# Tiles of three rows in four slots instead of four rows in three slots, in an instance norm that streams 2 GB through one core

## The chip, the core and the metric

One core of a Trainium2 chip runs the kernel alone. The metric is the device time of one execution in microseconds (us); less is better. "Median" is the median of a kernel's runs.

## The reference

```python
x: [256, 256, 4096] float32          # 65536 rows of 4096
mean = np.mean(x, axis=2, keepdims=True)
var = np.var(x, axis=2, keepdims=True)
out = (x - mean) / np.sqrt(var + eps)
```

Each row of 16 KB is read once (1073.74 MB in all), normalized and written once (1073.74 MB). There is no matrix product.

## The kernel before

A tile has 128 partitions with K = 4 consecutive rows each: 64 KB per partition, 8 MB in all, 128 tiles. The kernel keeps three such tiles ("slots") in SBUF. SyncE issues all DMAs, VectorE does the row sums and most scalings, ScalarE the squares, the square roots and three quarters of each tile's last row. This is the part that the change touches, cut:

```python
K = 4; BUFS = 3; Q = 3072
X = [pool.tile([P, K, d], fp32, name=f"x{s}") for s in range(BUFS)]

def vector_tile(s, r0=0, k=K, ...):
    take(V, ld, 16)                                  # the tile has landed
    for r in range(r0, r0 + k):                      # row sums (and x <- x/d)
        V.tensor_scalar(out=x[:, r, :], in0=x[:, r, :], scalar1=1.0 / d, ..., accum_out=mean[s][:, r:r+1]).then_inc(means, 1)
    for b in range(r0, r0 + k, 2):                   # two rows at a time
        ...                                          # wait for their square root
        mine(V.reciprocal(out=rstd..., in_=std...)); mine(V.scalar_tensor_tensor(out=nbias..., ...))
        for r in range(b, b + 2):                    # scale; of the last row only the columns from Q on
            f = slice(Q, d) if r == r0 + k - 1 else slice(0, d)
            V.tensor_scalar(out=x[:, r, f], in0=x[:, r, f], scalar1=rstd..., scalar2=nbias..., ...).then_inc(dn, 1)

def scalar_tile(s, r0=0, k=K, ...):
    for r in range(r0, last + 1):
        mine(A.activation(out=junk, in_=x[:, r, :], func=AF.Square, ..., accum_out=ss[s][:, c]))
        if (r - r0) % 2:                             # a square root for every two rows
            A.activation(out=std..., in_=ss..., func=AF.Sqrt, ...).then_inc(stds, 1)
    A.activation(out=x[:, last, :Q], in_=x[:, last, :Q], func=AF.Identity, ...).then_inc(dn, 1)
...
    # SyncE; the first and the last tile go in halves (cut)
    with S.Fori(0, rounds) as i:
        for t in range(L0, L0 + BUFS):
            store(t % BUFS, (t, BUFS, rounds, i))                 # waits until tile t is done
            load((t + 2) % BUFS, (t + 2, BUFS, rounds, i))        # waits until tile t-1 has been stored
```

The whole kernel:

## Time and profile before

| | before |
|---|---|
| median of the first 6 runs | 4963.06 us (4961.5 to 4963.66) |
| span of the profile | 4960.2 us |
| DMA queue: packets, share of the span | 37296, 100.0% |
| VectorE, ScalarE busy | 66%, 49% |
| one tile, from its load's landing to its store's issue | 26.4 us |

This is the timeline of the kernel before, in two cuts (start, duration, engine, line of the kernel, operation, output and input, count; then the idle time ahead of it and what ended it):

```profile
1004.27 0.34 SPq L165 DMA_DIRECT2D out_dram<-x  x1
1004.85 0.35 SPq L170 DMA_DIRECT2D x<-in_x_dram  x1
1016.84 4.42 DVE L87 TENSOR_SCALAR_CACHE_REDUCE x<-x 128x4096 f32<-128x4096 f32 x1 [12.72 <-DMA x<-in_x_dram]
...
1043.28 0.34 SPq L165 DMA_DIRECT2D out_dram<-x  x1
```

A load lands and the first sum starts at 1016.84; the tile's store is issued at 1043.28, 26.4 us later. Tiles follow each other every 38.6 us, so VectorE is idle for some 12 us of each.

### The profile page before, as it was taken

How to read it: one execution, taken by the hardware profiler on the slowest of the kernel's cores; microseconds unless marked ns; L12 is line 12 of the kernel's file. 1: busy time of each engine (PE TensorE's matmuls, PEld its weight loads, DVE VectorE, ACT ScalarE, POOL GpSimd, SP SyncE). 2: the span in 40 equal slices, each digit the busy share in tenths (PEclk: the TensorE clock that was granted, in tenths of full speed). 3: DMA queues.
4: the chain of work that ended last, by engine and by line, in shares of the span. 5: the costliest groups of instructions: out<-in, count | busy, mean ns of one | idle time of the engine just before them, and what ended most of it. 6: DMA issues, size and time to landing. Idle time of an engine off the chain costs nothing.

```text
span 4960.2 us, 5938 instructions
## 1 busy us (share of the span) xinstructions
DVE 3298.0 (66%) x2049; ACT 2407.7 (49%) x1412; POOL 0.2 (0%) x4
## 2 busy tenths in 40 slices
DVE  6666666666666666666666666666666666666666
ACT  4455444554445544455445544455444554445544
POOL 0000000000000000000000000000000000000000
DMA  9999999999999999999999999999999999999999
GB/s 422 431 435 433 431 435 433 432 437 432 432 438 432 433 437 432 433 437 432 435 435 432 436 434 431 438 433 431 438 433 432 438 432 433 438 432 433 438 432 405
DMA packets 37298, 2147.52 MB, mean 433 GB/s; under 512 B 4144, under 2 KB 4144, under 8 KB 4144
## 3 DMA queue, kind: packets, MB, share of 16 engines
q1 hardware_dynamic: 37296, 2147.50, 100.0%
q14 instruction: 2, 0.02, 0.0%
HBM read 1073.74 MB, written 1073.74 MB: 433 GB/s over the span
## 4 chain that ended last, share of the span: by engine, by line
DVE 62%; another core or an unknown queue 31%; issue 4%; DMA 2%; ACT 0%; DVEq 0%; ACTq 0%; SPq 0%
DVE x L87 44%; DVE x L112 17%; DMA x<-in_x_dram 1%; DVE nbias L100 1%; DMA out_dram<-x 1%; DVE rstd L98 1%; ACT junk L137 0%; DVEq L68 0%; DVEq L219 0%; ACT L146 0%; ACT std L146 0%; ACTq L68 0%; ACTq L67 0%; SPq L265 0%
## 5 line engine op out<-in xcount | busy, mean ns | idle before, releaser
L87 DVE TENSOR_SCALAR_CACHE_REDUCE x<-x 128x4096 f32<-128x4096 f32 x512 | 2232.3, 4416 | 1580.4 <-DMA x<-in_x_dram 1580.4
L137 ACT ACTIVATE junk<-x,mean 128x4096 f32<-128x4096 f32 x512 | 1883.1, 3678 | 2367.2 <-DVE x L87 2367.2
L112 DVE TENSOR_SCALAR x<-x,rstd,nbias 128x4096 f32<-128x4096 f32 (+1 forms) x512 | 1004.2, 2004 | 33.9 <-DVE nbias L100 29.3
L151 ACT ACTIVATE x<-x,nbias,rstd 128x3072 f32<-128x3072 f32 x130 | 383.2, 2948 | 146.2 <-DVEq L68 146.2
L137 ACT ACTIVATION_READ_ACCUMULATOR junk<-x,mean 128x1 f32 x512 | 95.5, 187 | 0.0
L146 ACT ACTIVATE std<-ss,eps_tile 128x2 f32<-128x2 f32 x256 | 75.6, 295 | 19.1
L98 DVE RECIPROCAL rstd<-std 128x2 f32<-128x2 f32 x256 | 40.7, 159 | 19.4 <-ACT std L146 19.4
L100 DVE SCALAR_TENSOR_TENSOR nbias<-mean,rstd 128x2 f32<-128x2 f32 x256 | 41.1, 161 | 8.9
L87 DVE DVE_READ_ACCUMULATOR x<-x 128x1 f32 x512 | 42.3, 83 | 0.0
L137 ACT ACT_TABLE_LOAD x1 | 1.3, 1283 | 1.2 <-DVE eps_tile L216 1.2
L146 ACT ACT_TABLE_LOAD x1 | 1.3, 1283 | 0.1
L216 DVE MEMSET eps_tile<- 128x1 f32 x1 | 0.1, 59 | 1.0 <-SPq L192 1.0
L251 POOL MEMSET const-bfloat16-1.0<- 128x1 bf16 x1 | 0.1, 101 | 0.0
L251 POOL MEMSET const-uint8-127<- 128x1 uint8 x1 | 0.1, 101 | 0.0
L251 POOL MEMSET const-float32-1.0<- 128x1 f32 x1 | 0.1, 99 | 0.0
L251 POOL MEMSET const-float32-0.0<- 128x1 f32 x1 | 0.1, 98 | 0.2 <-issue 0.2
## 6 DMA issues: line engine op xcount, KB each, us to landing
out_dram<-x SPq DMA_DIRECT2D x4, 4096.0 KB, 19.6
x<-in_x_dram SPq DMA_DIRECT2D x2, 4096.0 KB, 16.7
x<-in_x_dram SPq DMA_DIRECT2D x127, 50.3
out_dram<-x SPq DMA_DIRECT2D x126, 31.5
```

What stands on the lines that cost most here:

```text
L87: V.tensor_scalar(out=x[:, r, :], in0=x[:, r, :], scalar1=1.0 / d, scalar2=None, op0=ALU.mult, op1=ALU.add, accum_out=mean[s][:, r : r + 1 ...
L98: mine(V.reciprocal(out=rstd[s][:, c], in_=std[s][:, c]))
L100: mine(V.scalar_tensor_tensor(out=nbias[s][:, c], in0=mean[s][:, c], scalar=-1.0 / d, in1=rstd[s][:, c], op0=ALU.mult, op1=ALU.mult))
L112: V.tensor_scalar(out=x[:, r, f], in0=x[:, r, f], scalar1=rstd[s][:, c], scalar2=nbias[s][:, c], op0=ALU.mult, op1=ALU.add,).then_inc(dn, 1)
L137: mine(A.activation(out=junk, in_=x[:, r, :], func=AF.Square, bias=mean[s][:, c], scale=-float(d), accum_out=ss[s][:, c]))
L146: A.activation(out=std[s][:, c], in_=ss[s][:, c], func=AF.Sqrt, bias=eps_tile, scale=1.0 / d**3).then_inc(stds, 1)
L151: A.activation(out=x[:, last, :Q], in_=x[:, last, :Q], func=AF.Identity, bias=nbias[s][:, c], scale=rstd[s][:, c]).then_inc(dn, 1)
L216: V.memset(eps_tile, eps / d**2).then_inc(ready, 1)
L251: nc = _bacc.Bacc("TRN2", target_bir_lowering=False, num_devices=1)
```

## The change

Its intent: smaller tiles (three rows, 6 MB), a fourth slot, and loads three tiles ahead, so that more transfers are queued; 65536 rows make 170 such tiles and a last one of two rows. The first and last tile are no longer cut in halves. The work within a tile is simpler: one square root per tile, ScalarE scales the last row and VectorE the others. The core of the diff:

```diff
-    K = 4
-    BUFS = 3
-    Q = 3072
+    K = 3
+    BUFS = 4
+    AHEAD = 3
+    full = n // (P * K)
+    rest_k = n // P - full * K          # the last tile: two rows
@@ VectorE @@
-        for b in range(r0, r0 + k, 2):  ... (reciprocal, bias and scaling for two rows at a time)
+        take(V, stds, 1)
+        V.reciprocal(out=rstd[s][:, :k], in_=std[s][:, :k]).then_inc(own_v, 1)
+        ...
+        for r in range(k - 1):
+            V.tensor_scalar(out=x[:, r, :], in0=x[:, r, :], scalar1=rstd[s][:, c], scalar2=nbias[s][:, c], ...).then_inc(done[s], 1)
@@ ScalarE @@
-            if (r - r0) % 2:  ... (a square root for every two rows)
+        A.activation(out=std[s][:, :k], in_=ss[s][:, :k], func=AF.Sqrt, ...).then_inc(stds, 1)
-            out=x[:, last, :Q], in_=x[:, last, :Q], func=AF.Identity, ...
+            out=x[:, k - 1, :], in_=x[:, k - 1, :], func=AF.Identity, ...
@@ SyncE @@
-        ... (half loads and half stores of the first and the last tile)
+        for t in range(AHEAD):
+            load(t, t, wait=False)
+        for t in range(first):
+            store(t, t)
+            load(t + AHEAD, t + AHEAD, wait=False)
         with S.Fori(0, rounds) as i:
-            for t in range(L0, L0 + BUFS):
+            for t in range(first, first + BUFS):
                 store(t % BUFS, (t, BUFS, rounds, i))
-                load((t + 2) % BUFS, (t + 2, BUFS, rounds, i))
+                load((t + AHEAD) % BUFS, (t + AHEAD, BUFS, rounds, i))
```

More of the change, by code (lines that the diff above doesn't have):

```diff
@@ L19 @@
     fp32 = mybir.dt.float32
-    AX = mybir.AxisListType
     AF = mybir.ActivationFunctionType
@@ L30 @@
     n, d = x_flat.shape
-    assert n % (P * K) == 0 and d & (d - 1) == 0
-    ntiles = n // (P * K)
-    x_t = x_flat.rearrange("(t p k) d -> t p k d", p=P, k=K)
-    out_t = out_flat.rearrange("(t p k) d -> t p k d", p=P, k=K)
-    assert ntiles == 128
-    half = K // 2
+    assert d & (d - 1) == 0
+    full = n // (P * K)
+    rest_k = n // P - full * K
+    assert rest_k >= 2 and n % P == 0
+    ntiles = full + 1
+    cut = full * P * K
+    x_t = x_flat[:cut, :].rearrange("(t p k) d -> t p k d", p=P, k=K)
+    out_t = out_flat[:cut, :].rearrange("(t p k) d -> t p k d", p=P, k=K)
+    x_r = x_flat[cut:, :].rearrange("(p k) d -> p k d", p=P)
+    out_r = out_flat[cut:, :].rearrange("(p k) d -> p k d", p=P)
     pool = ctx.enter_context(tc.tile_pool(name="pool", bufs=1))
@@ L51 @@
     )
-    loaded = [nc.alloc_semaphore(f"loaded{s}") for s in range(BUFS + 1)]
-    stored = [nc.alloc_semaphore(f"stored{s}") for s in range(BUFS + 1)]
+    loaded = [nc.alloc_semaphore(f"loaded{s}") for s in range(BUFS)]
+    stored = [nc.alloc_semaphore(f"stored{s}") for s in range(BUFS)]
     own_v = nc.alloc_semaphore("own_v")
@@ L62 @@
     scaled = nc.alloc_semaphore("scaled")
-    done = [nc.alloc_semaphore(f"done{s}") for s in range(BUFS + 1)]
+    done = [nc.alloc_semaphore(f"done{s}") for s in range(BUFS)]
     ready = nc.alloc_semaphore("ready")
@@ L70, with vector_tile @@
     V, A, S = nc.vector, nc.scalar, nc.sync
-    def vector_tile(s, r0=0, k=K, ld=None, dn=None):
+    def vector_tile(s, k=K):
         x = X[s]
-        ld = loaded[s] if ld is None else ld
-        dn = done[s] if dn is None else dn
-        own = 0
-        def mine(instruction):
-            nonlocal own
-            own += 1
-            return instruction.then_inc(own_v, 1)
-        if ld:
-            take(V, ld, 16)
-        for r in range(r0, r0 + k):
+        take(V, loaded[s], 16)
+        for r in range(k):
             V.tensor_scalar(
@@ L90, in vector_tile @@
             ).then_inc(means, 1)
-        for b in range(r0, r0 + k, 2):
-            c = slice(b, b + 2)
-            final = b == r0 + k - 2
-            if final:
-                take(V, stds, (b - r0) // 2 + 1)
-            else:
-                V.wait_ge(stds, (b - r0) // 2 + 1)
-            mine(V.reciprocal(out=rstd[s][:, c], in_=std[s][:, c]))
-            V.wait_ge(own_v, own)
-            mine(V.scalar_tensor_tensor(
-                out=nbias[s][:, c], in0=mean[s][:, c], scalar=-1.0 / d, in1=rstd[s][:, c], op0=ALU.mult, op1=ALU.mult
-            ))
-            if final:
-                take(V, own_v, own)
-            else:
-                V.wait_ge(own_v, own)
-            if final:
-                V.sem_inc(scaled, 1)
-            for r in range(b, b + 2):
-                c = slice(r, r + 1)
-                f = slice(Q, d) if r == r0 + k - 1 else slice(0, d)
-                V.tensor_scalar(
-                    out=x[:, r, f], in0=x[:, r, f], scalar1=rstd[s][:, c], scalar2=nbias[s][:, c],
-                    op0=ALU.mult, op1=ALU.add,
-                ).then_inc(dn, 1)
@@ L117, in scalar_tile @@
-    def scalar_tile(s, r0=0, k=K, ld=None, dn=None):
-        x = X[s]
-        dn = done[s] if dn is None else dn
-        last = r0 + k - 1
-        own = 0
-        def mine(instruction):
-            nonlocal own
-            own += 1
-            return instruction.then_inc(own_a, 1)
-        for r in range(r0, last + 1):
+        take(V, stds, 1)
+        V.reciprocal(out=rstd[s][:, :k], in_=std[s][:, :k]).then_inc(own_v, 1)
+        V.wait_ge(own_v, 1)
+        V.scalar_tensor_tensor(
+            out=nbias[s][:, :k], in0=mean[s][:, :k], scalar=-1.0 / d, in1=rstd[s][:, :k], op0=ALU.mult, op1=ALU.mult
+        ).then_inc(own_v, 1)
@@ L130, in scalar_tile @@
+        take(V, own_v, 2)
+        V.sem_inc(scaled, 1)
+        for r in range(k - 1):
+            c = slice(r, r + 1)
+            V.tensor_scalar(
+                out=x[:, r, :], in0=x[:, r, :], scalar1=rstd[s][:, c], scalar2=nbias[s][:, c],
+                op0=ALU.mult, op1=ALU.add,
+            ).then_inc(done[s], 1)
+    def scalar_tile(s, k=K):
+        x = X[s]
+        for r in range(k):
             c = slice(r, r + 1)
-            if own:
-                A.wait_ge(own_a, own)
-            if r == last:
+            if r:
+                A.wait_ge(own_a, r)
+            if r == k - 1:
@@ L134, in scalar_tile @@
                 take(A, means, k)
             else:
-                A.wait_ge(means, r - r0 + 1)
-            mine(A.activation(
+                A.wait_ge(means, r + 1)
+            A.activation(
                 out=junk, in_=x[:, r, :], func=AF.Square, bias=mean[s][:, c], scale=-float(d), accum_out=ss[s][:, c]
-            ))
-            if (r - r0) % 2:
-                c = slice(r - 1, r + 1)
-                if r == last:
-                    take(A, own_a, own)
-                else:
-                    A.wait_ge(own_a, own)
-                A.activation(
-                    out=std[s][:, c], in_=ss[s][:, c], func=AF.Sqrt, bias=eps_tile, scale=1.0 / d**3
-                ).then_inc(stds, 1)
@@ L149, in scalar_tile @@
-        c = slice(last, last + 1)
+            ).then_inc(own_a, 1)
+        take(A, own_a, k)
+        A.activation(
+            out=std[s][:, :k], in_=ss[s][:, :k], func=AF.Sqrt, bias=eps_tile, scale=1.0 / d**3
+        ).then_inc(stds, 1)
+        c = slice(k - 1, k)
         take(A, scaled, 1)
         A.activation(
-            out=x[:, last, :Q], in_=x[:, last, :Q], func=AF.Identity, bias=nbias[s][:, c], scale=rstd[s][:, c]
-        ).then_inc(dn, 1)
-    def rows_of(ap, t):
+            out=x[:, k - 1, :], in_=x[:, k - 1, :], func=AF.Identity, bias=nbias[s][:, c], scale=rstd[s][:, c]
+        ).then_inc(done[s], 1)
@@ L157, in rows_of @@
+    def rows_of(ap, rest, t):
         if isinstance(t, int):
-            return ap[t]
+            return ap[t] if t < full else rest
         first, period, count, i = t
@@ L161, in rows_of, with rows_in @@
         return ap[bass.ds(i, 1)].rearrange("o p k d -> p (o k) d")
+    def rows_in(t):
+        return rest_k if t == full else K
     def store(s, t):
-        take(S, done[s], K + 1)
-        S.dma_start(out=rows_of(out_t, t), in_=X[s][:, :, :]).then_inc(stored[s], 16)
+        k = rows_in(t)
+        take(S, done[s], k)
+        S.dma_start(out=rows_of(out_t, out_r, t), in_=X[s][:, :k, :]).then_inc(stored[s], 16)
     def load(s, t, wait=True):
+        k = rows_in(t)
         if wait:
             take(S, stored[s], 16)
-        S.dma_start(out=X[s][:, :, :], in_=rows_of(x_t, t)).then_inc(loaded[s], 16)
@@ L172, in half_of @@
-    def half_of(h):
-        return slice(h * half, (h + 1) * half)
-    def second(sems, s, h):
-        return sems[BUFS] if h else sems[s]
-    def store_half(s, t, h):
-        r = half_of(h)
-        take(S, second(done, s, h), half + 1)
-        S.dma_start(out=out_t[t][:, r, :], in_=X[s][:, r, :]).then_inc(second(stored, s, h), 16)
-    def halves(tile_fn, s, first):
-        for h in range(2):
-            ld = second(loaded, s, h) if first or h == 0 else False
-            tile_fn(s, h * half, half, ld, second(done, s, h))
@@ L188 @@
-    last = ntiles - 1
-    rounds = (ntiles - 5) // BUFS
-    L0 = 2
-    with tc.tile_critical():
-        for h in range(2):
-            r = half_of(h)
-            S.dma_start(out=X[0][:, r, :], in_=x_t[0][:, r, :]).then_inc(second(loaded, 0, h), 16)
-        load(1, 1, wait=False)
-        store_half(0, 0, 0)
-        store_half(0, 0, 1)
-        load(2, 2, wait=False)
-        store(1, 1)
-        take(S, stored[BUFS], 16)
-        load(0, 3)
+        S.dma_start(out=X[s][:, :k, :], in_=rows_of(x_t, x_r, t)).then_inc(loaded[s], 16)
@@ L204 @@
+    first = BUFS - AHEAD
+    rounds = (full - AHEAD - first) // BUFS
+    tail = range(first + rounds * BUFS, ntiles)
+    with tc.tile_critical():
+        for t in range(AHEAD):
[3 more added lines that the diff above has]
+            load(t + AHEAD, t + AHEAD, wait=False)
         with S.Fori(0, rounds) as i:
-            for t in range(L0, L0 + BUFS):
+            for t in range(first, first + BUFS):
                 store(t % BUFS, (t, BUFS, rounds, i))
-                load((t + 2) % BUFS, (t + 2, BUFS, rounds, i))
@@ L208 @@
-        load(last % BUFS, last)
-        store((last - 2) % BUFS, last - 2)
-        store((last - 1) % BUFS, last - 1)
-        store_half(last % BUFS, last, 0)
-        store_half(last % BUFS, last, 1)
-        for s in ((last - 2) % BUFS, (last - 1) % BUFS, last % BUFS, BUFS):
-            take(S, stored[s], 16)
+                load((t + AHEAD) % BUFS, (t + AHEAD, BUFS, rounds, i))
+        for t in tail:
+            store(t % BUFS, t)
+            if t + AHEAD < ntiles:
+                load((t + AHEAD) % BUFS, t + AHEAD)
@@ L216 @@
+        for t in range(ntiles - BUFS, ntiles):
+            take(S, stored[t % BUFS], 16)
         V.memset(eps_tile, eps / d**2).then_inc(ready, 1)
-        halves(vector_tile, 0, True)
-        vector_tile(1)
+        for t in range(first):
+            vector_tile(t)
         with V.Fori(0, rounds) as i:
-            for j in range(BUFS):
-                vector_tile((L0 + j) % BUFS)
-        vector_tile((last - 2) % BUFS)
-        vector_tile((last - 1) % BUFS)
-        halves(vector_tile, last % BUFS, False)
+            for t in range(first, first + BUFS):
+                vector_tile(t % BUFS)
@@ L226 @@
+        for t in tail:
+            vector_tile(t % BUFS, rows_in(t))
         take(A, ready, 1)
-        halves(scalar_tile, 0, True)
-        scalar_tile(1)
+        for t in range(first):
+            scalar_tile(t)
         with A.Fori(0, rounds) as i:
-            for j in range(BUFS):
-                scalar_tile((L0 + j) % BUFS)
-        scalar_tile((last - 2) % BUFS)
-        scalar_tile((last - 1) % BUFS)
-        halves(scalar_tile, last % BUFS, False)
+            for t in range(first, first + BUFS):
+                scalar_tile(t % BUFS)
@@ L238 @@
+        for t in tail:
+            scalar_tile(t % BUFS, rows_in(t))
 _INS = ['x', 'eps']
```

## The prediction

> **What bounds the kernel now.** I read the page first, then the waits of the engines and of the DMA queue, then the windows, and last the single packet records of the trace. On the page the share of the span decides:
>
> ```profile
> span 4960.2 us, 5938 instructions
> DVE 3298.0 (66%) x2049; ACT 2407.7 (49%) x1412; POOL 0.2 (0%) x4
> ...
> DMA  9999999999999999999999999999999999999999
> ...
> DMA packets 37298, 2147.52 MB, mean 433 GB/s; under 512 B 4144, under 2 KB 4144, under 8 KB 4144
> ...
> q1 hardware_dynamic: 37296, 2147.50, 100.0%
> ```
>
> VectorE (DVE) works two thirds of the time and ScalarE (ACT) half of it, but the 16 DMA engines are busy for 100.0% of the span, from the first slice to the last. 4144 of the 37296 packets are the 4-byte completion marks (259 transfers x 16), which leaves 33152 = 259 x 128 data packets: one for each partition of each transfer, 64 KB in a whole tile and 32 KB in the half tiles at both ends.
>
> The chain of waits on the page looks different: it gives VectorE 62%. That is a trap here. The waits tell why:
>
> ```profile
> DVE x L87 <- DMA x<-in_x_dram: 1580.4, 126, 13.2
> ```
> ```profile
> SPq L68 <- DVE x L112: 4757.1, 130, 38.3
> SPq L68 <- DMA out_dram<-x: 47.7, 3, 30.7
> ```
>
> VectorE waits 12 to 13 us for a load in every tile (126 times), so it is not the limit. SyncE, which issues the DMAs, waits for VectorE (4757.1 us), and that would cost time only if the DMA queue ran empty meanwhile. The issues say that it does not:
>
> ```profile
> x<-in_x_dram SPq DMA_DIRECT2D x127, 50.3
> out_dram<-x SPq DMA_DIRECT2D x126, 31.5
> ```
>
> A tile's transfer takes 8 packets of 2.414 us on each engine (below) = 19.3 us. A store lands 31.5 us after its issue, so some 31.5 - 19.3 - 1.5 = 11 us of older work are still queued when it is issued (1.5 us: my estimate for start and completion; the first half load was issued at 0.96 us, its packets began at 1.98, ended at about 11.7, and its user started at 13.17). The load behind it tells the same: 50.3 - 2 x 19.3 - 1.5 = 10 us. The windows agree:
>
> ```profile
> 1000.00:2000.00 1000.00, 665.52 (x412) 483.12 (x283) 0.00 (x0) 1.00 1.00 434
> ```
>
> The last three columns are granted clock, DMA share and GB/s: share 1.00, 434 GB/s.
>
> [...] In the packet records, starts within one transfer are 2.414 us apart for 64 KB and 1.209 us for 32 KB. The difference, 1.205 us, is the price of 32 KB, and so 1.209 - 1.205 = 0.004 us is left per packet[...]. [...]
>
> **The change part by part.** The bytes stay: 1073.74 MB read and as much written.
>
> *Smaller packets.* Three rows per partition make 48 KB packets. I expect a spacing of 1.5 x 1.205 + 0.004 = 1.8115 us. Before, each engine moves 2024 packets of 64 KB and 48 of 32 KB with 259 completion marks, each of which delays the next packet by 0.006 us: 2024 x 2.414 + 48 x 1.209 + 259 x 0.006 = 4885.9 + 58.0 + 1.6 = 4945.5 us. After: 170 full tiles x 2 transfers x 8 = 2720 packets of 48 KB, 16 of 32 KB for the last tile, 342 marks: 4927.3 + 19.3 + 2.1 = 4948.7 us. **Plus 3.2 us**, on the path that sets the end.
>
> *The middle.* A pair of load and store takes 16 x 1.8115 = 29.0 us. VectorE has per tile 3 sums x (4.416 + 0.083 us), 0.32 of small work and 2 scalings x 2.37 (4.74 for two in the timeline) = 18.6 us, plus a bubble of about 4.5 us in which it waits for the square root of the last row (the half tiles, 4.52 us, show it undiluted): 23 us, below 29. ScalarE has 3 x (3.678 + 0.187) + 0.295 + one scaling of 4096 columns at about 3.68 = 15.6 us. Both stay hidden. The lost pairing of rows (one square root per tile, no ScalarE/VectorE split of the last row) costs nothing at the end of the program as long as the queue is full.
>
> *Three tiles ahead.* In queue order store t is four transfers (58 us) behind the end of load t, and it is issued some 25 us after that load's end (23 of work, the rest for completion). Load t+3 needs the slot of tile t-1, whose store ends two transfers before this load's turn, so it is issued some 27 us early. The queue before was 10 us deep at each issue; now it is 27 or more. But its share was 1.00 already, so **nothing is won**.
>
> *Start.* Before, two halves and one load are queued (39 us), and the first half store is issued at 31.54. After, three loads last until 2.0 + 24 x 1.8115 = 45.5 us. Tile 0 is usable at about 18; three sums to 31, square, table load and root to 36.8, small work, two scalings: store 0 issued at about 42.5, some 3 us ahead of an empty queue, with 1 us from issue to first packet. It just fits.
>
> *End.* Before, the last half store is issued at 4942.0, when ten of the engines have run dry for about 1.5 us (the packet records end at 4941 and begin again at 4942.5). After, the last tile has its load before the stores of tiles 168 and 169 in the queue: 29 us, in which its 20 us of work fit. Up to 1.5 us are won for those engines. But they are not the last: their packets end at 4952.3 and the slowest engine's at 4958.7, because some fell behind by up to 6.4 us on slow packets, nearly all in the first 1200 us, around changes from loads to stores, while the engines run in step.
>
> *Sum.* Begin of packets 2.0, packets 4948.7, losses of the slowest engine: before 4958.7 - 2.0 - 4945.5 = 11.2; I take 10 after. End at 4960.7, plus 1.5 to the end of the span = 4962; and the time is 2.8 us above the span before (4963.0 against 4960.2), so **4965 us**.
>
> **The rivals.** (1) *The deeper queue wins time.* For it speaks the 4757 us that SyncE waits for VectorE. Against it: the DMA share of 1.00 and the 10 us that are always queued. Its most is the 11 us of losses plus 1.5: about 4950 us, still within 2%. (2) *A new hole at start or end*: store 0 or the last store comes late, since a tile's work is no longer cut into halves. My margins are 3 and some 9 us; if I am wrong, each hole costs 3 to 10 us: 4968 to 4985. (3) *Compute becomes the bound*: only if a tile took over 29 us on VectorE, against 23; at 31 us it would be 171 x 31 = 5300 us. No row speaks for it. (4) *48 KB packets are treated worse*, for example cut at each row of 16 KB: then 8208 packets per engine with 0.004 each add some 25 us: 4990, again below 2%. (5) Another pitch in HBM changes the rate: no view shows a loss at 64 KB, so nothing is to be won, and a loss over 2% would need a rate below 425 GB/s.
>
> **Range and chances.** 2% is 99 us. No rival but (3) reaches that. The slowest engine's losses may be anything from 3 us (the fast engines' own) to 18, and a small hole may come: 4957 to 4976. Faster by over 2% would need 443 GB/s[...]: 0.5%. Slower: 1.5%. Same: 98%.
>
> **What would show each step.** Packets: 43776 data and 5472 marks on the DMA queue's row, spacing 1.81 us. DMA share 100%, middle windows at 433 to 434 GB/s. VectorE some 3170 us busy, ScalarE some 2660. The waits of SyncE turn round: some 19 us per tile for a store's landing (about 3200 us) and only about 9 us for compute. Issue to landing: stores about 49 us, loads about 44. Starts of sums 29.0 us apart from tile to tile. The prediction is wrong if a DMA slice of the first or last 50 us drops, if packets are not 48 KB, or if the period differs from 29.0 us.

The sum is 2.0 + 4948.7 + 10 = 4960.7 us, with 1.5 and 2.8 us on top 4965. The 0.004 us per packet in it is the measured 1.209 us less the 1.205 us by which 64 KB take longer than 32. That a better queue can win next to nothing in the steady state rests on the measured share of 1.00; the 0.5% for "faster" is my estimate. The 425 and 443 GB/s are the measured 433 and 434, 2% lower and higher.

## More of the kernel before

Every run told of here was classed as fast, with a granted clock of 1.0.

The profile is one more execution under the hardware profiler; its span, from the first instruction to the last, is some 1.7 us shorter than that execution's time.

The chain that ended last, on the page of the kernel before, would mislead a hurried reader:

```profile
DVE 62%; another core or an unknown queue 31%; issue 4%; DMA 2%; ACT 0%; DVEq 0%; ACTq 0%; SPq 0%
```

It follows waits back from the last instruction, and a store waits for VectorE; that the transfers ahead of this store were still in the DMA queue at that moment is no wait, so the chain does not see it.

## The result

| | before | after |
|---|---|---|
| median, 6 runs each | 4963.06 us | 4967.5 us (4966.07 to 4968.92) |
| ratio of the fast runs | 1 | 1.001, 95% interval 0.9997 to 1.0022: the same |
| span of the profile | 4960.2 us | 4964.7 us |

A ratio here is the mean time of one kernel's fast runs over that of the other's of the same rounds, so it is not quite the ratio of the medians quoted. The time lies 2.5 us above the predicted 4965 and inside the range.

The page of the kernel after, by the lines that the prediction read before:

```profile
span 4964.7 us, 6088 instructions
DVE 3101.8 (62%) x1708; ACT 2649.4 (53%) x1368; POOL 0.2 (0%) x4
...
DMA packets 49250, 2147.52 MB, mean 433 GB/s; under 512 B 5472, under 2 KB 5472, under 8 KB 5472
...
q1 hardware_dynamic: 49248, 2147.51, 100.0%
...
DMA 78%; DVE 16%; ACT 4%; issue 1%; another core or an unknown queue 0%; SPq 0%; DVEq 0%; ACTq 0%
```

49248 - 5472 = 43776 data packets, as predicted; the same bytes; the DMA queue again busy for 100.0%. The chain now names the DMA (78%), since SyncE waits for stores to land. The limit did not move from VectorE to the DMA: it was the DMA before, and only the chain's way of naming it changed. SyncE's own waits in the kernel after show the turn:

```profile
SPq L70 <- DMA out_dram<-x: 3308.4, 168, 21.0
SPq L70 <- DVE x L93: 1444.5, 170, 40.9
SPq L70 <- ACT x L118: 18.6, 1, 18.6
```

Before, it was 47.7 us for stores and 4757.1 us for VectorE. The issues of the kernel after (count, KB each, median us from issue to landing):

```profile
x<-in_x_dram SPq DMA_DIRECT2D x170, 6144.0 KB, 43.3
out_dram<-x SPq DMA_DIRECT2D x170, 6144.0 KB, 49.3
```

By the prediction's reckoning a store now waits for some 49.3 - 14.5 - 1.5 = 33 us in the queue ahead of its own 14.5 us; before it was some 11. The queue is deeper, and the rate is what it was, 434 GB/s from 1000 to 2000 us. The windows of the kernel after (the last three columns are clock, DMA share, GB/s):

```profile
1000.00:2000.00 1000.00, 625.82 (x343) 530.82 (x273) 0.00 (x0) 1.00 1.00 434
```

The packet records carry the rest. In the middle of the run the commonest distance from one packet's start to the next is 2.414 us for 64 KB before and 1.812 us for 48 KB after.

### The profile page after: what moved, and what is told of

Its sections match the earlier page's. It is cut to its first block, busy times and chain, and to the rows that moved or that the text cites. A ratio compares the mean times of both kernels' runs of the same rounds, so it can differ in the third digit from the quotient of the medians.

```text
span 4964.7 us, 6088 instructions
## 1 busy us (share of the span) xinstructions
DVE 3101.8 (62%) x1708; ACT 2649.4 (53%) x1368; POOL 0.2 (0%) x4
## 2 busy tenths in 40 slices
DMA packets 49250, 2147.52 MB, mean 433 GB/s; under 512 B 5472, under 2 KB 5472, under 8 KB 5472
## 3 DMA queue, kind: packets, MB, share of 16 engines
q1 hardware_dynamic: 49248, 2147.51, 100.0%
## 4 chain that ended last, share of the span: by engine, by line
DMA 78%; DVE 16%; ACT 4%; issue 1%; another core or an unknown queue 0%; SPq 0%; DVEq 0%; ACTq 0%
DMA out_dram<-x 41%; DMA x<-in_x_dram 37%; DVE x L79 12%; DVE x L93 4%; ACT junk L109 3%; ACT std L113 0%; DVE nbias L86 0%; DVE rstd L84 0%; DVEq L70 0%; ACT x L118 0%; SPq L142 0%; SPq L136 0%; ACTq L70 0%; SPq L70 0%
## 5 line engine op out<-in xcount | busy, mean ns | idle before, releaser
L93 DVE TENSOR_SCALAR x<-x,rstd,nbias 128x4096 f32<-128x4096 f32 x341 | 807.5, 2410 | 31.7 <-DVE nbias L86 31.7
L118 ACT ACTIVATE x<-x,nbias,rstd 128x4096 f32<-128x4096 f32 x171 | 650.1, 3802 | 122.7 <-DVEq L70 122.7
L84 DVE RECIPROCAL rstd<-std 128x3 f32<-128x3 f32 x171 | 30.0, 175 | 774.5 <-ACT std L113 774.5
L113 ACT ACTIVATE std<-ss,eps_tile 128x3 f32<-128x3 f32 x171 | 50.7, 296 | 19.8
L86 DVE SCALAR_TENSOR_TENSOR nbias<-mean,rstd 128x3 f32<-128x3 f32 x171 | 27.6, 162 | 5.9
## 6 DMA issues: line engine op xcount, KB each, us to landing
x<-in_x_dram SPq DMA_DIRECT2D x170, 6144.0 KB, 43.3
out_dram<-x SPq DMA_DIRECT2D x170, 6144.0 KB, 49.3
```

Source lines behind the costliest of these rows:

```text
L84: V.reciprocal(out=rstd[s][:, :k], in_=std[s][:, :k]).then_inc(own_v, 1)
L86: V.scalar_tensor_tensor(out=nbias[s][:, :k], in0=mean[s][:, :k], scalar=-1.0 / d, in1=rstd[s][:, :k], op0=ALU.mult, op1=ALU.mult).then_in ...
L93: V.tensor_scalar(out=x[:, r, :], in0=x[:, r, :], scalar1=rstd[s][:, c], scalar2=nbias[s][:, c], op0=ALU.mult, op1=ALU.add,).then_inc(done ...
L113: A.activation(out=std[s][:, :k], in_=ss[s][:, :k], func=AF.Sqrt, bias=eps_tile, scale=1.0 / d**3).then_inc(stds, 1)
L118: A.activation(out=x[:, k - 1, :], in_=x[:, k - 1, :], func=AF.Identity, bias=nbias[s][:, c], scale=rstd[s][:, c]).then_inc(done[s], 1)
```

## The experiments

Three of the quantities come from the single records in the traces, and are used in the tables below:

- **Slow packets**: data packets that took over 0.06 us more than the median of their size (2.418 us for 64 KB, 1.815 for 48 KB, 1.213 for 32 KB, 0.611 for 16 KB). Their excess is summed and divided by 16, so it is time per DMA engine.
- **Lag**: a transfer ends with 16 completion marks, one from each DMA engine (4144 for the 259 transfers of the kernel before, 5472 for the 342 of the changed one). The lag is the time from the first of a transfer's marks to the last: how far the latest engine is behind the foremost.
- **Left**: what the foremost engine still has queued when a store is issued. It is about the store's time from issue to landing, less its own transfer, less the lag. Read straight from the packet records, as the time from a store's issue to the end of the transfer ahead on the foremost engine, it is some 0.4 us less: in the median 4.4 us in the kernel before, 27.6 in the changed one, 1.2 in the three-slot kernel below.

### What a packet costs: rows padded apart, and tiles of two rows

The first edit keeps the schedule and turns each 48 KB packet into three of 16 KB:

```diff
-    X = [pool.tile([P, K, d], fp32, name=f"x{s}") for s in range(BUFS)]
+    X = [pool.tile([P, K, d + 4], fp32, name=f"x{s}")[:, :, :d] for s in range(BUFS)]
```

> The changed kernel with rows padded by 16 bytes in SBUF, so that a partition's three rows are three packets of 16 KB instead of one of 48 KB; the schedule is the same. Theory (each packet costs 0.004 us beside its bytes): 131072 data packets, spacing 0.606 us, 8192 per engine, so 4969.7 against 4948.7 us of packets, and 4988 us (4981 to 4997). Rival A (packets have no cost of their own here; the 4 us of the change come from elsewhere, as from stragglers): 4967 again. Rival B (the cost is the 0.0085 us by which a packet's own duration exceeds its bytes): about 5013.

Measured: 4994.66 us (ratio 1.0067 to the kernel before, 1.0054 to 1.008). The page of this run:

```profile
DMA packets 136546, 2147.52 MB, mean 430 GB/s; under 512 B 5472, under 2 KB 5472, under 8 KB 5472
```

131072 data packets, as meant. Their commonest distance is 0.607 us, and 8192 x 0.607 = 4972.5 us per engine, 25.9 us more than the 8 x 340 x 1.8115 + 16 x 1.209 = 4946.6 us of the changed kernel; measured against its 4967.5 us the time is 27.2 us longer. The expectation had 4969.7 us of packets and marks; with 0.607 and 342 marks of 0.006 it is 4974.6, which is 4.9 of the 6.7 us by which its 4988 was too low. Rival B's 0.0085 us is the 0.611 us that a packet of 16 KB lasts in the records, less 0.6025 for its bytes (half of the 1.205 for 32 KB); its 5013 us did not come.

The second edit is `K = 2`, six slots, five tiles ahead (and `full` one less, so that the last tile has two rows as well):

> The changed kernel with two rows per tile, six slots, five ahead: 32 KB packets, 512 transfers. Theory: 4096 packets x 1.209 + 512 x 0.006 = 4955.2 us, 6.5 more than the changed kernel; the work per tile of 16 us stays below the 19.3 us of a load and a store: 4974 us (4967 to 4982), middle windows near 433.5. Rival (deeper lookahead or smaller tiles win at the ends more than the packets cost): below 4965.

Measured: 4973.94 us (1.0024, 1.0011 to 1.0037), as the theory had it. In four kernels the distances are 2.414, 1.812, 1.209 and 0.607 us for 64, 48, 32 and 16 KB: 1.205 us per 32 KB and 0.004 to 0.005 us per packet. Both are read from the packet records of these kernels. That the smaller packets cost what I said is shown.

### What the fourth slot and the third tile ahead are for

The edit takes them away; the start is kept by loading all three slots at once:

```diff
-    BUFS = 4
-    AHEAD = 3
+    BUFS = 3
+    AHEAD = 2
@@
-        for t in range(AHEAD):
+        for t in range(BUFS):
             load(t, t, wait=False)
         for t in range(first):
             store(t, t)
-            load(t + AHEAD, t + AHEAD, wait=False)
```

> The changed kernel with three slots and loads two tiles ahead (all three slots are loaded at the start, so the start is the same). Theory (the extra tile of lookahead is worth nothing in the steady state, because 29 us of queue cover 24.5 us of work): middle windows stay at 433 to 434 GB/s, packets 49248; the last store comes some 8 us late, so about 4975 us (4968 to 4985). Rival A (the fourth slot is what fills the queue): the windows fall below 430 GB/s and the time rises over 5010. Rival B (the queue's reserve of 4.5 us is smaller than the spread of the engines, keeps them in step, and each change from load to store goes on costing the late ones 0.2 to 0.6 us per tile): 5000 to 5060, with slow packets through the whole run and not only in the first 1200 us.

Measured: 5071.41 us, 2.2% slower than the kernel before (1.0221, 1.0208 to 1.0234). My theory fell. Two lines of the page of the run (the second is a store's time from issue to landing) and then a window of it:

```profile
q1 hardware_dynamic: 49248, 2147.51, 99.7%
...
out_dram<-x SPq DMA_DIRECT2D x170, 6144.0 KB, 20.6
```
```profile
1000.00:2000.00 1000.00, 614.13 (x339) 523.05 (x271) 0.00 (x0) 1.00 1.00 426
```

This is a trap worth seeing: the DMA engines are busy for 99.7% of the span, yet move 426 instead of 434 GB/s. They hardly stand idle; single packets take longer. There are 2900 slow packets against 135 in the changed kernel, together 86.8 us per engine against 3.7, and 2114 of them come after 1500 us, where the changed kernel has none. A packet with a completion mark right behind it is the last of its transfer on that engine. Of the 2114, 982 are the last of a store, mostly on the foremost engines (33.7 us per engine in sum), 342 the last of a load, mostly on late engines (12.6 us), and the rest lie elsewhere, many of them first packets (16.8 us). In the kernels before and after, by contrast, most slow packets are the last of a load (145 of 172 and 113 of 135). Rival B of the expectation is thus right that slow packets go on through the whole run, somewhat above the 5060 us that it allowed; late engines going from a load to a store, which it named, are the smaller part of them. (To its 0.2 to 0.6 us: in the kernel before, nine in ten of the slow packets after 100 us exceed the median by 0.08 to 0.70 us.)

The next run tells the slots from the lookahead: four slots, loads two ahead.

```diff
-    AHEAD = 3
+    AHEAD = 2
@@ (three loads queued at the start, as in the changed kernel) @@
```

> The changed kernel with its four slots, but loads only two tiles ahead (three loads are queued at the start, so the start is the same). It tells the slots from the lookahead. Theory (what counts is how much work is queued when a store is issued, 4.4 us as in the first experiment, and not how many slots there are): 5055 to 5085 us, lag of the latest engine held at 4 to 5 us, slow packets to the end. Rival (the fourth slot itself makes the difference): 4966 to 4980.

Measured: 5065.07 us (1.0184, 1.0141 to 1.0227, so by the rule at 2% unclear; three runs of the kernel before in these rounds took 5004 to 5008 us, and by the medians it is 2.1%), 2947 slow packets, lag 4.4 to 5 us. A window of it:

```profile
1000.00:2000.00 1000.00, 615.99 (x339) 524.03 (x271) 0.00 (x0) 1.00 1.00 426
```

It is the three-slot kernel's time with four slots: the fourth slot itself does nothing, and what counts is how much is queued when a store is issued.

### The rewritten program with the old tiles

`K = 4`, three slots, two ahead in the changed program, all three slots loaded at the start, whole tiles at both ends:

> The new, simpler program with the old tiles: four rows, three slots, two ahead, whole tiles at both ends. It tells the tile's size from the rest of the rewriting. Theory: 64 KB packets again, 4945.4 us of them; the start is covered by three queued loads (58 us against a first store at 54); at the end the last store of 8 MB is issued 31 us after its load and the store ahead of it lasts 19.3, so the DMA engines stand idle for some 12 us: 4975 us (4968 to 4983), a dip in the last windows. Rival (whole tiles at the ends cost nothing, and the 4 us of the change are all packets): 4962 to 4965.

Measured: 5026.16 us, and one of six runs took 4980.55 (ratio 1.0108, 1.0081 to 1.0136). The profile is of one of the five longer runs (5027.21 us). Windows of it, an early and a late one:

```profile
200.00:800.00 600.00, 384.68 (x200) 296.51 (x153) 0.00 (x0) 1.00 1.00 433
1200.00:4800.00 3600.00, 2285.68 (x1196) 1775.62 (x919) 0.00 (x0) 1.00 1.00 429
```

It starts at full rate and loses it. The idle at the end was sized right: the latest engine ran dry at 4992.9 us and the last store's packets began at 5004.5, 11.6 us later against 12 expected. What the theory's 4975 us lacked was the same effect as above (1412 slow packets after 1500 us); the one run at 4980.55 is near it. In this program a tile takes 29.9 us from landing to store (2000.05 to 2029.91 in its timeline), against 26.4 in the kernel before with the same tiles and slots: the pairs of rows and the split last row of the kernel before are worth 3.5 us of reserve.

### The kernel before with whole tiles at its ends

```diff
-        for h in range(2):   ... (half loads of tile 0)
-        store_half(0, 0, 0)
-        store_half(0, 0, 1)
+        load(0, 0, wait=False); load(1, 1, wait=False); load(2, 2, wait=False)
+        store(0, 0)
@@
-        store_half(last % BUFS, last, 0)
-        store_half(last % BUFS, last, 1)
+        store(last % BUFS, last)
```

> The kernel before with whole tiles instead of halves at both ends; its pairs of rows and its split last row stay, so that a tile takes 26.4 us from load to store against 29.9 in the rewritten program with the same tiles and slots. Theory (the pairs and the split keep the reserve of the three-slot queue at 10 us, and that is what keeps the engines out of step; the halves only cover the ends): no slow packets after some 1200 us, about 12 us of idle at the end, 4975 us (4967 to 4984). Rival (the halves at the start set the engines out of step, and the pairs are worth nothing): 5010 to 5035, as the rewritten program with four rows.

Measured: 4962.32 us against 4962.3 for the kernel before (1.0, 0.9987 to 1.0013), and no slow packet after 1500 us. The pairs and the split thus do keep the rate; and the halves are worth nothing. My 12 us of idle at the end were wrong: this program issues its last load ahead of the store of tile 125, so two stores (38.6 us) and not one lie between that load and the last store. The packet records show nine engines idle for 1.1 to 4.0 us ahead of the last store, and the late ones not at all. The changed program issues its last load one store later.

### Shorter work in three slots

The three-slot kernel of the first experiment again, with wrong results, so that only the time from a load to its store shrinks:

```diff
-                out=x[:, r, :], in0=x[:, r, :], scalar1=rstd[s][:, c], ...      # VectorE's scaling
+                out=x[:, r, :1024], in0=x[:, r, :1024], scalar1=rstd[s][:, c], ...
-            out=x[:, k - 1, :], in_=x[:, k - 1, :], func=AF.Identity, ...       # ScalarE's scaling
+            out=x[:, k - 1, :1024], in_=x[:, k - 1, :1024], func=AF.Identity, ...
```

> The three-slot kernel of the first experiment with scalings of 1024 columns instead of 4096, wrong results on purpose: the DMA pattern, slots and code stay, and only the time from a load to its store shrinks, by about 3.4 us (two scalings of 4.74 us become about 1.3). The queue's reserve grows from some 4.4 to 7.8 us. Theory (the loss of 104 us came from a reserve so small that the fast engines wait for the slow ones and all 16 stay in step): slow packets stop after some 1200 us, middle windows at 433 to 434 GB/s, the engines' last packets lie several us apart again, 4972 us (4964 to 4985). Rival (three slots of 48 KB are slow by themselves, by the pattern of transfers): it stays at 5060 to 5080.

Measured: 5031.63 us: 40 us better than with full work and still far from full rate. 1746 slow packets came after 1500 us. The lag grew to 7.6 us and stayed there; left is 1.6 us. A tile takes 19.96 us from its first sum to its store (1004.76 to 1024.72 in the timeline) against 23.14 in the three-slot kernel (2019.92 to 2043.06). So 3.2 us more of reserve let the lag grow by some 3 us, and it met the end of the queue again. My idea of how much reserve is enough was too small. The next step also cuts the sums and squares to 2048 columns:

> Three slots again, wrong results on purpose: the scalings of 1024 columns of the fifth experiment and now also sums and squares of 2048 columns. A tile's time from load to store shrinks by some 8 us more, so that the reserve of the queue grows from 7.8 to about 16 us. The fifth run kept its slow packets with its latest engines 7.7 us behind the first, which is its reserve. Theory (slow packets end once the late engines have fallen 5.5 to 7.5 us behind, as in the kernels before and after; a reserve below or at that holds the fast engines back every tile, and then they never end): with 16 us the lag settles at 5 to 8 us, slow packets stop after some 1200 us, the middle windows show 434 GB/s, 4966 us (4960 to 4976). Rival (three slots, or a load that need not wait for a store's landing, are slow whatever the reserve): over 5010.

Measured: 4977.09 us. Against the kernel before the ratio is 1.0004 (0.9962 to 1.0046), but three runs of that kernel in these rounds took 5004 to 5008 us (below); by the medians it is 15 us slower. The theory's 4966 was missed, and the run shows why within itself. Its windows:

```profile
2000.00:2800.00 800.00, 231.66 (x270) 211.41 (x216) 0.00 (x0) 1.00 1.00 433
2800.00:3200.00 400.00, 120.12 (x140) 109.62 (x112) 0.00 (x0) 1.00 1.00 434
3200.00:4800.00 1600.00, 471.93 (x550) 430.62 (x440) 0.00 (x0) 1.00 1.00 432
```

| this run, around | lag, us | left for the foremost engine, us |
|---|---|---|
| 400 us | 4.8 | 12.3 |
| 1200 us | 7.1 | 10.1 |
| 2000 us | 10.2 | 7.0 |
| 3000 us | 13.9 | 3.3 |
| 4000 us | 15.2 | 2.0 |

From 1000 to 3000 us there are 8 slow packets, from 3200 to 4800 us 413. In between nothing changed in the program. One engine fell behind by a steady 0.37 us in 100 us, and the reserve shrank by as much. From 1000 to 3000 us a store was issued 3.3 to 10.6 us before the foremost engine ended the transfer ahead; after 3400 us it was 1.5 to 1.8 us, no more than that engine's last packet, and slow packets came back, on the foremost engines and on others. The engines hardly stood idle for it: the gaps from 3400 to 4800 us sum to 1.3 us per engine. This is the clearest evidence: the same kernel, in one execution, before and after the lag meets the end of the queue. It shows when the slow packets come back; why a packet is then slow it does not show.

### Engines set apart at the start

Three small loads at the very start, of 4, 8 and 12 partitions with 32 KB each, were to set the engines apart before the first change from loads to stores, in the changed kernel and in the kernel before. I meant them to fall on as many engines, so that four groups start some 1.2 us after one another (my estimate, from 1.209 us for a packet of 32 KB). The records do not name the engines, so where the loads fell is not shown:

```diff
+        for j in range(3):
+            p = slice((0, 4, 12)[j], (4, 12, 24)[j])
+            S.dma_start(out=X[BUFS - 1][p, :2, :], in_=x_t[BUFS - 1][p, :2, :]).then_inc(shifted[j], 16)
```

> The changed kernel with three small loads at the very start[...], into a slot not yet in use[...]. Theory (late engines lose 0.2 to 0.6 us at a change from load to store while they are nearly in step with the rest, and nothing once they are apart): of the 16 slow packets at the first change few are left, and the sum of slow packets falls from 4.2 to under 3 us per engine; the time stays within 0.15% of the changed kernel, 4960 to 4970[...]. Rival (slow packets have nothing to do with step): as many slow packets as before and 4968 to 4972.

> The kernel before with the same three small loads at the start. Theory: fewer slow packets in the first 1200 us than without (5.0 us per engine), 4958 to 4966 us. Rival (no connection): 4964 to 4968, the slow packets as many as before.

Measured: 4977.61 us (4977.33 to 4979.24) for the changed kernel, and 5017.13 us for the kernel before, of whose six runs two took 4974 and four 5015 to 5027. As a way to have fewer slow packets it failed: the start itself became slow (8 us per engine of slow packets in the first 60 us), and at the next changes from loads to stores the engines had slow packets again. What the first change costs once engines are apart stays open.

As a disturbance it told more than it was made for. The same disturbance costs the changed kernel 10 us once, in each run. It pushes the kernel before over its edge in four runs of six, one of which is the profiled one (5022.78 us). Windows of it:

```profile
200.00:800.00 600.00, 389.67 (x242) 281.18 (x165) 0.00 (x0) 1.00 1.00 433
1200.00:4800.00 3600.00, 2373.28 (x1475) 1724.95 (x1014) 0.00 (x0) 1.00 1.00 429
```

### All of them together

At about 2000 us of each profile (lag and left are medians over some twelve transfers):

| kernel | median us | lag | left | slow packets after 1500 us | slow packets in all, us per engine |
|---|---|---|---|---|---|
| before | 4963.06 | 7.5 | 4.7 | 2 | 4.4 |
| before again (next section) | 4961.71 | 8.5 | 3.7 | 3 | 4.8 |
| before, whole ends | 4962.32 | 6.2 | 6.0 | 0 | 4.8 |
| after | 4967.5 | 6.6 | 28.1 | 0 | 3.7 |
| after again (next section) | 4967.66 | 7.2 | 27.5 | 0 | 3.8 |
| after, packets of 16 KB | 4994.66 | 4.9 | 30.2 | 0 | 2.2 |
| after, set apart | 4977.61 | 5.9 | 28.8 | 3 | 10.7 |
| two rows, five ahead | 4973.94 | 5.5 | 22.8 | 1 | 3.0 |
| three slots | 5071.41 | 4.7 | 1.6 | 2114 | 86.8 |
| four slots, two ahead | 5065.07 | 4.6 | 1.7 | 2177 | 83.8 |
| three slots, short work | 5031.63 | 7.6 | 1.6 | 1746 | 65.6 |
| rewritten, four rows | 5026.16 | 7.5 | 1.7 | 1412 | 49.7 |
| before, set apart | 5017.13 | 10.2 | 2.2 | 1309 | 55.8 |

Every kernel here with 1.6 to 2.2 us left goes on having slow packets to the end (1309 to 2177 after 1500 us); every one with 3.7 or more has next to none after 1500 us (0 to 3). Neither the number of slots nor the size of a tile sorts them so. In the profiles of both kernels the engines' last packets end up to 6 and 10 us apart (before 4952.3 to 4958.7 us, after 4953.3 to 4963.1). That the three-slot kernel's end within 0.1 us (5065.5 to 5065.6) is no sign of the effect: its last store was issued when all engines had run dry (its packets began at 5055.7, 4.2 us after the last ones before), so they all began it together.

### Both kernels again

> The changed kernel once more, on the chip of the two runs beside it, to compare with them and to see its spread. Both theories: 4966 to 4969 us, 0.1% above the kernel before, no run above 4975.

> The kernel before against itself, unchanged. Four of its 40 runs so far took 4993 to 5008 us, all others 4961 to 4967, and none of the changed kernel's 12 left 4964 to 4971. Theory (its queue's reserve of 10 us lies just above the lag of 7.5 to 8.3 us that its latest engines reach, so that now and then the lag meets the reserve and slow packets do not end): again mostly 4961 to 4964, with about one run in ten at 4990 to 5010; if the profile falls into such a run, it shows a latest engine some 10 us behind and slow packets late in the run. Rival (the four runs were disturbances from outside): no run above 4970, or such runs of other lengths.

Measured: the changed kernel 4967.66 us (4963.98 to 4970.64), the kernel before 4961.71 us (4961.28 to 4962.54) and, in the runs beside it, once 5003.37. The changed kernel's ratio to the kernel before was 0.9985 (0.9943 to 1.0027) in its rounds, in which three runs of the kernel before took 5004 to 5008.

In all, 57 runs of the kernel before were made. 52 took 4961 to 4967 us, five took 4993, 5003, 5004, 5004 and 5008. Twelve of the changed kernel took 4964 to 4971. That the five are the lag meeting the end of the queue fits (the kernel before has 3.7 to 4.7 us left, and its disturbed version shows that state at 5017), but none of the five was profiled, so it is argued and not shown. With none of twelve against five of 57, it is not shown either that the changed kernel never does it.

## Why the prediction was right, point by point

- **The bound.** Right. The DMA queue is at 100.0% before and after, 434 GB/s in the middle of both.
- **Smaller packets, plus 3.2 us.** Right, and shown twice by itself: predicted distance 1.8115 us, measured 1.812; 16 KB and 32 KB packets gave, to some 7 us and less than 1, the times that the same two numbers give. (Rival (4) has a slip: rows of 16 KB make 8192 packets per engine and not 8208.)
- **The middle.** Right where it said that work stays hidden. Issue to landing was predicted at 49 and 44 us and came to 49.3 and 43.3; SyncE's waits at 3200 us for stores and 9 us per tile for compute came to 3308.4 and (1444.5 for VectorE + 18.6 for ScalarE) / 170 = 8.6. VectorE was busy for 3101.8 us instead of 3170, since I added 42 us of read-outs of the accumulator (512 of 0.083 us) that overlap the next instruction (both start at 1021.19 in the timeline of the kernel before), and the sums, 4.42 us long, start 4.34 us apart and so overlap each other by another 25 us; ScalarE's scaling took 3.80 instead of 3.68 us.
- **"Nothing is won" by three tiles ahead.** Right as a sentence on the time against the kernel before, and wrong as a reading of what the lookahead is for. With it removed, the same tiles take 5065 to 5071 us. What I compared was the queue's depth with the length of a tile's work. What was missing is that the 16 engines do not run in step here: the latest is 5 to 10 us behind in the table above, a tile's work starts only after the last of its load's 16 marks (0.14 us after it at 1016.84 us before and at 1011.02 after), and the queue must also cover that. The 10 or 11 us that the prediction has queued at each store were the latest engine's; the foremost had 4.4. (The 1.5 us taken off there for start and completion was also too much: the first half load's packets ended at 12.2 to 12.6 us, not at 11.7.) The kernel before covers it by short work per tile (26.4 us), the changed kernel by lookahead, having given up the short work. The two parts cancel in the time.
- **Start and end.** At the start right: the first store was issued at 43.25 us against 42.5 predicted, and the three loads' packets lasted until 46.6 on the first engine, against 45.5 predicted. At the end it fit by luck: of the margin of some 9 us nothing was left, since the last load landed on the latest engine some 10 us after the foremost; seven engines stood idle for 0.2 to 0.6 us ahead of the last store. It cost no time, since the latest engine sets the end; from 4900 to 4950 us the rate is 433 GB/s. The half tiles that the change gave up were worth nothing, as the kernel with whole ends shows.
- **The sum.** Here two terms were mis-sized in opposite directions, by 2.4 and 1.1 us, and partly cancel. "I take 10 after" for the losses of the slowest engine was 4963.1 - 2.0 - 4948.7 = 12.4 us. Their cause was also only half right: the prediction has them on slow packets of the first 1200 us, but 3.3 us of the 12.4 are the steady falling behind of one engine after 3000 us, without a single slow packet (the last section tells of it). And "the time is 2.8 us above the span before" set a median against the span of one profile; for the same execution it was 4961.97 - 4960.2 = 1.8 us, and 1.7 after. The profiled execution itself took 4966.37 us.
- **Rival (1)**, the deeper queue wins time, is refuted for the usual run. Rivals (2) to (5) did not come: no new hole over 0.6 us, 23 us of work, packets of 48 KB, full rate.

## What to carry to other kernels

Here, with the DMA queue full (100.0% of the span, 434 GB/s in the middle) before and after, deeper buffering and smaller tiles moved the time by little more than the cost of packets, 0.004 to 0.005 us each. But measure the reserve against the latest engine and not against the first: take a store's time from issue to landing, and subtract its own transfer and the spread of the completion marks. The kernels here that had 1.6 to 2.2 us left at 2000 us, about a packet's time (1.8 or 2.4 us), took 5017 to 5071 us, one of them at a DMA share of 99.7%. Before a change that seems to bring nothing is judged, take its parts away one by one: a lookahead of three tiles, with the fourth slot that it needs, wins nothing against the old kernel and yet is what makes the rest of the change affordable. No version here beats both kernels; what is left above the packets' own time is mostly the losses of the slowest engine: in the changed kernel's profiled execution 12.4 of 4966.37 - 4948.7 = 17.7 us.

## What the records show of the 16 DMA engines

All of this is read from the packets and completion marks in the profiles of these runs.

- The engines drift apart in one stream of loads and stores: at 2000 us the latest was 4.6 to 10.2 us behind in the kernels of the table. Where the queue reached only 1.6 us beyond that spread (three slots), rate was lost that hardly showed as idle time: 426 against 434 GB/s at a share of 99.7%, with 86.8 us per engine of slow packets.
- Most slow packets lay at the change from one transfer to the next: at the first change from a load to a store the load's last packet took 3.4 to 4.2 us instead of 2.418 on all 16 engines in the kernel before. In the three-slot kernel, with 1.6 us left, the change from a store to a load has more of them (982 against 342 after 1500 us). Why a packet is slow there stays open.
- One engine of 16 fell behind steadily: in the changed kernel its lag grew by 0.4 us in every 203 us (0.2%), from 6.6 us at 3000 us to 10.0 at 4700. Sorted by how far behind they are, the marks show such an engine from early on, hidden at first among the others: in the kernel before it is 1.9 us behind at 1203 us, 3.3 at 1995, 4.8 at 2999 and 6.5 at 4004. The trace does not name the engine, and why it falls behind is not shown.
